# Two feed-forward down products: 16 of 22 k tiles by seven products in place of 8, with PSUM tiles of two banks

## The chip, the cores and the metric

The kernel runs on one core of one Trainium2 chip. The metric is the device time of one execution in microseconds, the median of three runs. A core has five engines with an instruction stream each: TensorE (PE, matmuls; PEld is its weight load), VectorE (DVE), ScalarE (ACT), GpSimd (POOL) and SyncE (SP). The last three also issue DMAs. Matmuls write to PSUM, eight banks of 512 fp32 numbers in each of 128 partitions; everything else lives in SBUF.

## The reference

One transformer block for 512 positions of width 1024, in fp32:

```
x = x + 0.5 * ffn(rmsnorm(x), up1, down1)        # FFN1
x = x + mixer(rmsnorm(x))                        # convolution and gated linear attention
x = x + 0.5 * ffn(rmsnorm(x), up2, down2)        # FFN2
return rmsnorm(x)

def ffn(y, up, down):                            # d_ff = 2816
    g, u = split(y @ up)                         # [512, 2816] each
    return (silu(g) * u) @ down                  # [512, 2816] @ [2816, 1024]
```

The change is about `@ down`, whose contraction has 2816/128 = 22 k tiles.

## The kernel before

**Precision.** A matmul of fp32 accuracy is made of three float32r products: every operand is split into a rounded part (`hi`) and the residue (`lo`), and hi·hi, hi·lo and lo·hi are added up in PSUM. Splitting a weight tile of 128 x 1024 takes a cast on ScalarE (`wh`, L358) and a subtraction on VectorE (`wl`, L359).

**Weights.** `Weights` streams all weights in the order of two lists, `PLAN` (tiles) and `STEPS` (uses). Each tile of 512 KB is fetched by SP's queue (L329) into the pool `f`; `take` returns the split tile of the next step and `issue` prepares two steps ahead. `wh` has three buffers, so the cast of a step waits until TensorE has done with a step three back.

**Seven products.** A 2 x 2 block product is computed by seven block products in place of eight (the Strassen–Winograd form), named m1, p2, q6, p5, q7, p3, p4. They need sums of weight blocks and of operand blocks. The weight sums are made by accumulating DMAs on POOL's queue (L333) and on VectorE (L343). The operand sums, in class `Operands`, are made on VectorE, and each operand is then split by L599 (ScalarE) and L600 (VectorE); `make` does that for one product. Class `Set` runs the seven products of one set on three banks: `a` takes p2, `b` takes m1, then q6, q7 and p4, which add onto what stands there, and `c` takes p5 and p3. Intermediate values that are used again (m1, q6, q7) are copied out of PSUM by ScalarE (L556) when their product ends. One product in a set is 24 matmuls of 256 columns (L551). `run_sets` takes the sets in a staggered order: the m1 of the next set comes between q7 and p4 of a set.

**Where it is used.** In the up products of both FFNs (9 sets each), in the mixer (12 sets and a tall one, L627), in 8 of the 22 k tiles of FFN1's down product (2 sets), and in 8 of the 22 of FFN2's. The rest goes by plain tiles: one k tile is 8 x 3 = 24 matmuls of 512 columns. FFN1's down product is 12 plain tiles (L386 to L388), two sets, and 2 plain tiles at the end (`TAIL1`). FFN2's is `last_down`, whose output has positions on the partitions: 10 plain tiles (L833 to L835), seven products of 24 matmuls of 512 columns (L884) in the order `CHUNK_ORDER`, and 4 plain tiles (`TAIL`). There each product uses two banks, and each result is added from PSUM into `X` by VectorE (`add`, L842). The evictions of the last tiles are L903.

**PSUM.** Pool `ps` has six tiles of one bank each, handed out by `MM()`; pool `pa` has two, handed out by `AUX()`. The order of the instructions on each engine comes from a scheduler that takes what is ready by the program's dependencies, tile by tile.

Of the kernel before, what the change touches and what calls it, by code (L numbers as in the profile page):

```python
# [42 lines left out]
TAIL1 = 2  # L43

# [70 lines left out]
def sets(mat, pairs):  # L115
    firsts = []
    for cols in pairs:
        firsts.append(len(PLAN))
        PLAN.extend((mat, 4 * j, 4, (c,), HW) for c in cols for j in range(2))
    STEPS.extend(order(firsts))  # L120
# [29 lines left out]
CHUNK_ORDER = ("m1", "p2", "q6", "p5", "q7", "p3", "p4")  # L150
CHUNK_STEP = {}


def last_plan(down):
    us = full(down, KF)
    units(us[CHUNK : KF - TAIL])
    firsts = []
    for s in range(2):
        firsts.append(len(PLAN))
        PLAN.extend((down, 4 * j + 2 * s, 2, (512 * i,), 512) for i in range(2) for j in range(2))  # L160
    CHUNK_STEP.update({(s, p): len(STEPS) + 2 * i + s for i, p in enumerate(CHUNK_ORDER)
                       for s in range(2)})
    STEPS.extend((n, p) for p in CHUNK_ORDER for n in firsts)
    units(us[KF - TAIL :])


def ffn_plan(up, down, plain, slow):

    units(group(up, KD, (0, DFF, P, DFF + P), slow))
    for f in range(2, plain):  # L170
        units(single(up, KD, f * P))
        units(single(up, KD, DFF + f * P))
    sets(up, [(s * HW, DFF + s * HW) for s in range(plain // 2, KF // 2)])
    if slow:
        us = full(down, KF)
        units(us[CHUNK : KF - TAIL1])
        sets(down, [(2 * s * HW, (2 * s + 1) * HW) for s in range(D // (2 * HW))])
        units(us[KF - TAIL1 :])
    else:
        last_plan(down)  # L180
    ENDS.append(len(STEPS))
# [34 lines left out]
def block_kernel(ctx: ExitStack, tc: tile.TileContext, xT, vecs, gf, gup, wgl, wts, out):  # L216
# [6 lines left out]
    ps = ctx.enter_context(tc.tile_pool(name="ps", bufs=6, space=bass.MemoryType.PSUM))  # L223
# [20 lines left out]

    def MM():
        cnt[0] += 1
        return ps.tile([P, S], F32, tag="mm", name=f"mm{cnt[0]}")
# [27 lines left out]
    class Weights:  # L275
# [14 lines left out]
        def phase(self, early, first=6):  # L290
# [4 lines left out]
            for i in range(lo, self.end):  # L295
                n, p = STEPS[i]
                if p == "m1" and i in CHUNK_STEP.values():
                    at = CHUNK_STEP[0, "m1"]
                    self.loads.setdefault(at - (4 if i == at else 2), []).append(n)
                    self.sums.setdefault(i, []).append(n)  # L300
# [9 lines left out]
            if self.end == len(STEPS):  # L310
                c = CHUNK_STEP
                for i, at in enumerate((c[1, "q6"], c[1, "p3"], c[1, "p3"], c[1, "p4"])):
                    self.pre.setdefault(at, []).append(STEPS[self.end - TAIL + i][0])
# [21 lines left out]
        def issue(self):  # L335
# [4 lines left out]
            for n in self.sums.get(at, ()):  # L340
                self.raw[n].append(tile_of("f", [P, 1024]))
                a11, a12, a21, a22, s3 = self.raw[n]
                nc.vector.tensor_tensor(out=s3, in0=a11, in1=a21, op=ALU.add)  # L343
                self.add(a21, a22)
# [6 lines left out]
            else:  # L351
                a11, a12, a21, a22, s3 = (self.raw[n] + [None])[:5]
# [174 lines left out]
    class Set:  # L527
# [9 lines left out]
        def run(self, p):  # L537
            b = {"m1": "b", "p2": "a", "q6": "b", "p5": "c", "q7": "b", "p4": "b", "p3": "c"}[p]
            fresh = b not in self.bank
# [19 lines left out]

    class Operands:  # L560
# [5 lines left out]
        def __init__(self, b):  # L566
            self.b = b
            self.parts = {}
            self.sums = set()
# [20 lines left out]
        def make(self, p):  # L590
# [5 lines left out]
            v = self.sum(p)  # L596
            h, l = (tile_of("op", [P, 1024], F32R) for _ in range(2))
# [5 lines left out]
        def get(self, p):  # L603
            return self.parts[p]

    class Tall:
# [7 lines left out]
        def run(self, p, s):  # L614
            b = {"p2": "a", "p5": "c", "p3": "c"}.get(p, "b")
            fresh = b not in self.bank
            if fresh:
                self.bank[b] = [MM(), MM()]
# [38 lines left out]
    def ffn(up, down, norm, nxt, plain, at):  # L657
# [28 lines left out]
        xo = Operands(normed)  # L686

        def plain_pair(f, g, u):
# [4 lines left out]
            mul(hid[:, f], s, t)  # L693
# [13 lines left out]

        def up_set(i):
            h = hid[:, plain + 2 * i : plain + 2 * i + 2]

            def done(s, p):
# [6 lines left out]
                if p == "q7":  # L718
                    u2 = T()
                    nc.vector.scalar_tensor_tensor(out=u2, in0=bank["c"], scalar=-1.0, in1=v["q7"],  # L720
                                                   op0=ALU.mult, op1=ALU.subtract)
                    s.u2 = u2
                if p == "p4":
                    nc.vector.scalar_tensor_tensor(
                        out=h[:, :, :HW], in0=pair(bank["b"]), scalar=-1.0, in1=pair(s.g1),
                        op0=ALU.mult, op1=ALU.mult)
                if p == "p3":
                    g2 = T()
                    nc.vector.tensor_tensor(out=g2, in0=bank["c"], in1=v["q6"], op=ALU.add)
# [24 lines left out]
        def banks():  # L754
            return [AUX(), AUX()] + [MM() for _ in range(KD - 2)]

        def mm(d, k, w, hl):
            c = slice(d * P, (d + 1) * P)
            mm3(o[d], w[0][:, c], w[1][:, c], hl[0][:, k % 2], hl[1][:, k % 2],
                k in (CHUNK, KF - TAIL1), k in (KF - TAIL1 - 1, KF - 1))  # L760
# [6 lines left out]
        ho = Operands(lambda j, l: hid[:, 4 * j : 4 * j + 4, l * HW : (l + 1) * HW])  # L767
        o = banks()
        hls = {k: split_hid(k) for k in (CHUNK, CHUNK + 2)}
        more = [4, 6, 8, 10, "m1", "p2", "p5", "q6", "q7", "p3"]  # L770
        for k in range(CHUNK, KF - TAIL1):
# [3 lines left out]
            if more:  # L775
                n = more.pop(0)
                if isinstance(n, int):
                    hls[CHUNK + n] = split_hid(CHUNK + n)
                else:
                    ho.make(n)  # L780
        for d in range(KD):
            add_half(d)
        ho.make("p4")
# [7 lines left out]
        def down_set(i):  # L791
            def done(s, p):
                for l, a, by in uses[p]:
                    xt = X[:, 4 * i + 2 * a : 4 * i + 2 * a + 2, l * HW : (l + 1) * HW]
# [4 lines left out]
            return Set(ho, done, keep=())  # L799

        run_sets(down_set)
# [18 lines left out]
    def last_down(us, hid, split_hid):  # L820
# [6 lines left out]

        o = [[MM(), MM()] for t in range(NTB - 1)] + [[AUX(), AUX()]]

        def mm(t, e, k, w, hl):  # L830
            wh, wl = (a[:, 512 * e : 512 * (e + 1)] for a in w)
            a, b = (v[:, k % 2, t * P : (t + 1) * P] for v in hl)
            nc.tensor.matmul(o[t][e], a, wh, start=k in (CHUNK, KF - TAIL), stop=False)  # L833
            nc.tensor.matmul(o[t][e], a, wl, start=False, stop=False)  # L834
            nc.tensor.matmul(o[t][e], b, wh, start=False, stop=k in (KF - TAIL - 1, KF - 1))  # L835
# [9 lines left out]
        ho = Operands(lambda j, l: hid[:, 4 * j : 4 * j + 4, l * HW : (l + 1) * HW])  # L845
        hls = {k: split_hid(k) for k in (CHUNK, CHUNK + 2)}
        more = [4, 6, 8, "m1", "p2", "p5", "q6", "q7", "p3"]
        for k in range(CHUNK, KF - TAIL):
            w = W.take(us[k])
            for t in range(NTB):  # L850
                for e in range(2):
                    mm(t, e, k, w, hls[k - k % 2])
            if more:
                n = more.pop(0)
                if isinstance(n, int):
                    hls[CHUNK + n] = split_hid(CHUNK + n)
                else:
                    ho.make(n)
# [3 lines left out]
        ho.make("p4")  # L862
# [6 lines left out]
        for p in CHUNK_ORDER:  # L869
            b = {"p2": "a", "p5": "c", "p3": "c"}.get(p, "b")  # L870
            fresh = b not in banks
            if fresh:
                banks[b] = [MM(), MM()]
            bh, bl = ho.get(p)
            for s in range(2):
                h, l = W.take()
                for i in range(2):
                    k = 2 * s + i
                    wh, wl = (a[:, 512 * i : 512 * (i + 1)] for a in (h, l))
                    for e in range(2):  # L880
                        c = slice(k * HW + e * P, k * HW + (e + 1) * P)
                        to = banks[b][e]
                        for n, (aa, ww) in enumerate(((bh, wh), (bh, wl), (bl, wh))):
                            nc.tensor.matmul(to, aa[:, c], ww,  # L884
                                             start=fresh and k == 0 and n == 0,
                                             stop=k == 3 and n == 2, skip_group_check=True)
# [618 lines left out]
```

## Time and profile before

| | us |
|---|---|
| median of three runs (1194.18 to 1195.4) | 1195.39 |
| the profiled execution | 1195.04 |
| its span, first to last instruction | 1193.3 |
| TensorE busy | 1183.7 |
| VectorE busy | 841.7 |
| ScalarE busy | 591.7 |
| GpSimd busy | 106.4 |

The span is what the trace covers; the profiled execution's own time holds 1.7 us more. Busy times of engines overlap. What sets the time is the chain of work that ended last, and an engine's idle time matters only where this chain runs through it. "Clock" is the TensorE clock that was granted, with 1 for full speed; it was 0.998 on average here.

### The profile page before, as it was taken

The numbers are of one execution on the slowest core, as the hardware profiler recorded it, in microseconds if no ns is written. First come the engines' busy times: TensorE is split into PE (matmuls) and PEld (weight loads), VectorE is DVE, ScalarE is ACT, GpSimd is POOL, SyncE is SP. The second block draws the span as 40 slices with busy tenths as digits, with TensorE's granted clock in tenths as the row PEclk, the third lists the DMA queues.
The fourth block names the chain that finished last, engine by engine and source line by source line (L and its number), as shares of the span: only waits on it lengthen the run. The fifth ranks groups of instructions, "written<-read, shape, count | busy, mean of one in ns | idle before, by whom it ended". The sixth has DMA issues, their size and how long they took to land.

```text
span 1193.3 us, 19134 instructions
## 1 busy us (share of the span) xinstructions
PE 1183.7 (99%) x7834; PEld 1091.4 (91%) x7834; DVE 841.7 (71%) x1010; ACT 591.7 (50%) x736; POOL 106.4 (9%) x143
## 2 busy tenths in 40 slices
PE   9999999999999999999999999999999999999997
PEld 8899999988988889999999998888889999998886
DVE  7976666854787976667787786555597656675675
ACT  6554454622452746464554574334355555562353
POOL 0011111000110110101111100100001111100100
PEclk9999999999999999999999999999999999999999
DMA  9477777633482767778666766602637777763431
GB/s 345 82 210 183 189 177 190 182 89 90 99 278 72 172 158 208 196 185 212 143 152 147 189 172 214 203 18 78 213 81 211 170 184 173 185 174 117 92 92 70
DMA packets 58471, 190.80 MB, mean 160 GB/s; under 512 B 6576, under 2 KB 10800, under 8 KB 58384
## 3 DMA queue, kind: packets, MB, share of 16 engines
q1 hardware_dynamic: 36912, 124.27, 30.5%
q0 software_dynamic: 16832, 60.83, 27.5%
q10 hardware_dynamic: 4640, 4.49, 1.2%
q8 instruction: 61, 1.00, 0.3%
q14 instruction: 26, 0.21, 0.1%
HBM read 124.55 MB, written 8.39 MB: 111 GB/s over the span
## 4 chain that ended last, share of the span: by engine, by line
PE 97%; DVE 2%; issue 1%; ACT 0%; POOL 0%; DVEq 0%; ACTq 0%; POOLq 0%
PE mm L551 52%; PE mm L410 7%; PE mm L388 6%; PE mm L386 6%; PE mm L387 6%; PE mm L627 3%; PE mm L884 3%; PE mm L834 2%; PE mm L835 2%; PE mm L833 2%; PE aux L1173 1%; DVE wl L359 1%; PE aux L386 1%; PE aux L835 1%; PE aux L388 1%; PE aux L834 1%
## 5 line engine op out<-in xcount | busy, mean ns | idle before, releaser
L551 PE MATMUL mm<-op,wh 128*128 128x256 f32 x3584 | 648.8, 284 | 0.0
L358 ACT CAST wh<-f 128x1024 fp32r<-128x1024 f32 (+1 forms) x325 | 339.4, 1046 | 459.0 <-PE mm L551 221.8
L551 PEld LDWEIGHTS mm<-op,wh 128*128 128x128 f32 x3584 | 559.0, 192 | 1.1
L359 DVE TENSOR_TENSOR wl<-f,wh 128x1024 fp32r<-128x1024 f32 (+1 forms) x325 | 394.8, 1219 | 210.9 <-ACT wh L358 205.9
L551 PE MATMUL mm<-op,wl 128*128 128x256 f32 x1792 | 507.5, 283 | 0.9 <-DVE wl L359 0.9
L551 PEld LDWEIGHTS mm<-op,wl 128*128 128x128 f32 x1792 | 343.3, 192 | 1.6 <-DVE wl L359 1.5
L333 POOL DMA_DIRECT2D f<-f x108 | 93.4, 867 | 932.1 <-DVE wl L359 483.1
L386 PE MATMUL mm<-op,wh 128*128 128x512 f32 x340 | 132.3, 389 | 0.0
L387 PE MATMUL mm<-op,wh 128*128 128x512 f32 x340 | 132.3, 389 | 0.0
L388 PE MATMUL mm<-op,wl 128*128 128x512 f32 x340 | 132.3, 389 | 0.0
L387 PEld LDWEIGHTS mm<-op,wh 128*128 128x128 f32 x340 | 63.8, 188 | 13.3
L388 PEld LDWEIGHTS mm<-op,wl 128*128 128x128 f32 x340 | 63.8, 188 | 13.2
L386 PEld LDWEIGHTS mm<-op,wh 128*128 128x128 f32 x340 | 63.8, 188 | 13.2
L410 PE MATMUL mm<-op,wh 128*128 128x512 f32 x256 | 64.5, 394 | 0.0
L410 PEld LDWEIGHTS mm<-op,wh 128*128 128x128 f32 x256 | 48.6, 190 | 10.4
L556 ACT COPY tp<-mm 128x512 f32<-128x512 f32 x90 | 52.2, 580 | 2.0 <-DVE tp L1323 2.0
L599 ACT CAST op<-hid 128x1024 fp32r<-128x1024 f32 x28 | 29.4, 1051 | 37.4 <-PE aux L834 20.7
L600 DVE TENSOR_TENSOR op<-hid,op 128x1024 fp32r<-128x1024 f32 x28 | 34.2, 1222 | 17.7 <-ACT op L599 17.6
L343 DVE TENSOR_TENSOR f<-f,f 128x1024 f32<-128x1024 f32 x36 | 44.0, 1223 | 0.8
L627 PE MATMUL mm<-wh,op 128*128 128x512 f32 x112 | 34.9, 389 | 0.0
L884 PE MATMUL mm<-wh,op 128*128 128x512 f32 x112 | 34.6, 389 | 0.0
L410 PE MATMUL mm<-op,wl 128*128 128x512 f32 x128 | 34.2, 389 | 0.0
(252 smaller groups left out, 1107.7 us busy)
## 6 DMA issues: line engine op xcount, KB each, us to landing
f<-wts SPq DMA_DIRECT2D x219, 512.0 KB, 4.4
f<-f POOLq DMA_DIRECT2D x108, 512.0 KB, 5.0
X<-xT SPq DMA_DIRECT2D x8, 256.0 KB, 5.3
xs<-X POOLq DMA_DIRECT2D x8, 256.0 KB, 5.5
ga<-tp ACTq DMA_DIRECT2D x8, 256.0 KB, 5.3
gb<-tp ACTq DMA_DIRECT2D x8, 256.0 KB, 5.3
tp<-ga SPq DMA_DIRECT2D x8, 256.0 KB, 5.9
tp<-gb SPq DMA_DIRECT2D x8, 256.0 KB, 3.0
```

Source lines behind the costliest of these rows:

```text
L333: nc.gpsimd.dma_start(out_, a, accum_op=ALU.add)
L343: nc.vector.tensor_tensor(out=s3, in0=a11, in1=a21, op=ALU.add)
L358: nc.scalar.copy(h[:, :w], raw[:, :w])
L359: nc.vector.tensor_tensor(out=l[:, :w], in0=raw[:, :w], in1=h[:, :w].bitcast(F32), op=ALU.subtract)
L386: nc.tensor.matmul(o, wh, ah, start=first, stop=False)
L387: nc.tensor.matmul(o, wh, al, start=False, stop=False)
L388: nc.tensor.matmul(o, wl, ah, start=False, stop=last)
L410: nc.tensor.matmul(o[c], w[:, s : s + P], a[k], start=k == 0 and j == 0, stop=k == kt - 1 and j == 2)
L551: nc.tensor.matmul(to, ww[:, s], aa[:, t], start=fresh and k == 0 and e == 0 and j == 0, stop=k == 3 and j == 2, skip_group_check=True)
L556: nc.scalar.copy(v, o)
L627: nc.tensor.matmul(self.bank[b][e], aa[:, c], ww, start=fresh and i == 0 and n == 0, stop=k == 3 and n == 2, skip_group_check=True)
L884: nc.tensor.matmul(to, aa[:, c], ww, start=fresh and k == 0 and n == 0, stop=k == 3 and n == 2, skip_group_check=True)
```

## The change

**FFN1's down product**: 4 plain tiles (`FILL1`), then two chunks of 8 k tiles by seven products (4 sets), then 2 plain ones. The operands of the second chunk, and the last three of the first, are made by hooks in the sets.

**The last down product**: 2 plain tiles (`FILL`), two chunks of 8 by seven products, 4 plain ones. The products come in a new order (`chunk_order`). Operand sums are accumulating DMAs on POOL's queue, from one part of `hid` to another (class `Signed`, L715); what must be subtracted is made with a negative sign, either in `hid` when it is written (`negative`) or when the operand is split. The evictions of p2, p3, q7 and p4 (all but the last p4) are done by `far`: ScalarE scales the bank into a tile (L1003), and an accumulating DMA on POOL's queue adds it to `X` (L1004, 256 KB). The others stay with VectorE (`add`, L997).

**PSUM**: pool `ps` has three tiles of two banks each, and `MM()` hands out their halves one after the other.

The rest of the diff is a mode `joint`, which is switched off in every place, and the forms that it needs.

```diff
+FILL1 = 4
-CHUNK_ORDER = ("m1", "p2", "q6", "p5", "q7", "p3", "p4")
+FILL = 2
+CHUNKS = 2
+def chunk_order():
+    seq = [(0, "m1"), (0, "p2")]
+    for c in range(CHUNKS):
+        seq += [(c, p) for p in ("p5", "p3", "q6", "q7")]
+        seq += [(c + 1, "m1"), (c, "p4"), (c + 1, "p2")] if c + 1 < CHUNKS else [(c, "p4")]
+    return seq
...
-    ps = ctx.enter_context(tc.tile_pool(name="ps", bufs=6, space=bass.MemoryType.PSUM))
+    ps = ctx.enter_context(tc.tile_pool(name="ps", bufs=3, space=bass.MemoryType.PSUM))
+    half_bank = []
+    def MM2():
+        cnt[0] += 1
+        half_bank.clear()
+        return ps.tile([P, 2, S], F32, tag="mm", name=f"mm{cnt[0]}")
     def MM():
-        cnt[0] += 1
-        return ps.tile([P, S], F32, tag="mm", name=f"mm{cnt[0]}")
+        if half_bank:
+            return half_bank.pop()
+        t = MM2()
+        half_bank.append(t[:, 1])
+        return t[:, 0]
...
-                self.raw[n].append(tile_of("f", [P, 1024]))
-                a11, a12, a21, a22, s3 = self.raw[n]
-                nc.vector.tensor_tensor(out=s3, in0=a11, in1=a21, op=ALU.add)
+                a11, a12, a21, a22 = self.raw[n]
+                if STEPS.index((n, "p2")) > STEPS.index((n, "q7")):
+                    self.raw[n].append(tile_of("f", [P, 1024]))
+                    nc.vector.tensor_tensor(out=self.raw[n][4], in0=a11, in1=a21, op=ALU.add)
                 self.add(a21, a22)
...
+                if p == "q7" and s3 is a11:
+                    nc.vector.tensor_tensor(out=a11, in0=a11, in1=a22, op=ALU.subtract)
...
+    class Signed(Operands):
+        ORDER = ("m1", "p2", "p5", "p3", "q6", "q7", "p4")
+        SUMS = {"m1": [((0, 0), (0, 1))], "p5": [((0, 0), (1, 1)), ((0, 1), (1, 1))],
+                "q6": [((1, 0), (0, 0))]}
+        def make(self, p):
...
+            if p in ("p2", "q6"):
+                nc.scalar.activation(hv, v, AF.Copy, scale=-1.0)
+                nc.vector.scalar_tensor_tensor(out=lv, in0=v, scalar=-1.0, in1=hv.bitcast(F32),
+                                               op0=ALU.mult, op1=ALU.subtract)
...
+            for to, a in self.SUMS.get(p, ()):
+                nc.gpsimd.dma_start(self.b(*to), self.b(*a), accum_op=ALU.add)
...
+            for l in range(2):
+                c = slice(l * HW, (l + 1) * HW)
+                nc.vector.scalar_tensor_tensor(out=hid[:, f, c], in0=s[:, c],
+                                               scalar=-1.0 if negative(f, l) else 1.0,
+                                               in1=t[:, c], op0=ALU.mult, op1=ALU.mult)
...
-        more = [4, 6, 8, 10, "m1", "p2", "p5", "q6", "q7", "p3"]
-        for k in range(CHUNK, KF - TAIL1):
+        more = ["m1", "p2", "p5", "q6"]
+        for k in range(FILL1):
...
+        makes = [(0, "q7"), (0, "p3"), (0, "p4")] + [(1, p) for p in Operands.ORDER]
+        run_sets(down_set, hooks={(i, p): [make] for i, ps in
+                                  ((0, ("m1", "q6", "q7")), (1, ("m1", "q6", "p5", "q7", "p4")),
+                                   (2, ("q6", "q7"))) for p in ps})
...
+        def far(t, e, bank, by):
+            xt = X[:, 4 * e : 4 * e + 4, t * P : (t + 1) * P]
+            v = T()
+            nc.scalar.activation(v, bank, AF.Copy, scale=by)
+            nc.gpsimd.dma_start(xt, blocks(v), accum_op=ALU.add)
...
             for l, e, by in uses[p]:
                 for t in range(2):
-                    add(2 * l + t, e, banks[b][t], by)
+                    (far if p in ('p2', 'p3', 'p4', 'q7') and (c, p) != seq[-1] else add)(2 * l + t, e, banks[b][t], by)
```

**How instructions move: TensorE in FFN1's up sets.** The place is the end of q7 of one set. In the rows, `mm` is a PSUM tile, `op` an operand (hi or lo), `wh` and `wl` the parts of a weight tile; the brackets hold the engines and DMA queues whose semaphores the instruction waits for. Before, `mm_718` is bank `b` of the set and `mm_946` that of the next set:

```order
484 L551 MATMUL mm_718<-op_605,wl_847 128x256
485 L551 MATMUL mm_946<-op_358,wh_877 128x256 [waits PE_49]
486 L551 MATMUL mm_946<-op_359,wh_877 128x256
487 L551 MATMUL mm_946<-op_358,wl_878 128x256 [waits DVE_49]
488 L551 MATMUL mm_946<-op_358,wh_877 128x256
489 L551 MATMUL mm_946<-op_359,wh_877 128x256
```

The m1 of the next set goes on for 24 matmuls, and p4 of the set (`mm_718` again, which waits for ScalarE) follows.

After, `mm_935` holds the banks `b` and `a` of the set, `mm_1091` its bank `c` and the next set's `b`, `mm_1221` the bank `a` of the next set's p2, and `wh_1161` that product's weights:

```order
615 L587 MATMUL mm_935<-op_596,wl_1062 128x256
616 L587 MATMUL mm_1221<-op_368,wh_1161 128x256 [waits Activation_49]
617 L587 MATMUL mm_1221<-op_369,wh_1161 128x256
618 L587 MATMUL mm_935<-op_666,wh_1129 128x256 [waits Activation_49]
619 L587 MATMUL mm_935<-op_667,wh_1129 128x256
620 L587 MATMUL mm_935<-op_666,wl_1130 128x256 [waits DVE_49]
```

Two matmuls of the next p2 stand between q7 and p4 now; the next m1 (into `mm_1091`) comes behind the first 12 matmuls of p4, when VectorE has read bank `c`. On ScalarE the cast of `wh_1161` is ahead of the copy of q7 for which p4 waits:

```order
76 L392 CAST wh_1129<-f_676 128x1024 [waits DMAHW5_49,PE_49,Activation_49]
77 L392 CAST wh_1161<-f_897 128x1024 [waits DMAHW7_49,DVE_49,PE_49]
78 L592 COPY tp_1157<-mm_935 128x512 [waits PE_49]
79 L392 CAST wh_1192<-f_672 128x1024 [waits DMASW1_49,DVE_49,PE_49]
80 L592 COPY tp_1190<-mm_1091 128x512 [waits DVE_49,PE_49]
```

Both the cast and the copy wait for TensorE, and the copy's turn comes after the cast.

**How instructions move: POOL in the last down product.** Before, POOL's queue ends with weight sums for the seven products (`f<-f`):

```order
134 L333 DMA f_11026<-f_11028 128x1024 [waits DMAHW2_49,DMAHW1_49,DMAHW7_49,DVE_49,Activation_49]
135 L333 DMA f_10949<-f_10953 128x1024 [waits DMASW6_49,DMAHW3_49,DMASW2_49,DVE_49]
136 L333 DMA f_11022<-f_11026 128x1024 [waits DMAHW7_49,DMASW7_49,DVE_49]
137 L333 DMA f_10951<-f_10949 128x1024 [waits DMAHW4_49,DMASW0_49,DVE_49]
138 L333 DMA f_11024<-f_11022 128x1024 [waits DMAHW0_49,DMASW1_49,DVE_49]
```

After, in the first chunk (`hid<-hid` are operand sums, `X<-tp` evictions: of p2 in rows 155 and 156, of p3 in rows 160 and 161):

```order
153 L715 DMA hid_8623<-hid_8623 128x4x256 [waits DMASW6_49,DVE_49]
154 L715 DMA hid_8623<-hid_8623 128x4x256 [waits DMASW6_49]
155 L1004 DMA X_7915<-tp_11089 128x4x128 [waits Activation_49]
156 L1004 DMA X_7915<-tp_11092 128x4x128 [waits DMASW1_49,PE_49,Activation_49]
157 L364 DMA f_11053<-f_11055 128x1024 [waits DMAHW6_49,DMAHW5_49,DVE_49]
158 L715 DMA hid_8623<-hid_8623 128x4x256 [waits DVE_49]
159 L715 DMA hid_8623<-hid_8623 128x4x256 [waits DMASW4_49,DMASW3_49]
160 L1004 DMA X_7915<-tp_11180 128x4x128 [waits DMASW5_49,Activation_49]
161 L1004 DMA X_7915<-tp_11183 128x4x128 [waits PE_49,Activation_49]
```

Operand sums, evictions and weight sums share one queue now, and a weight sum and two operand sums, each with waits of its own, stand ahead of p3's eviction.

More of the change, by code (lines that the diff above doesn't have):

```diff
@@ L175, in ffn_plan @@
         us = full(down, KF)
-        units(us[CHUNK : KF - TAIL1])
-        sets(down, [(2 * s * HW, (2 * s + 1) * HW) for s in range(D // (2 * HW))])
+        units(us[:FILL1])
+        sets(down, [(2 * s * HW, (2 * s + 1) * HW) for s in range(D // (2 * HW))],
+             range(FILL1, KF - TAIL1, CHUNK))
         units(us[KF - TAIL1 :])
@@ L617, in run @@
             if fresh:
+                half_bank.clear()
                 self.bank[b] = [MM(), MM()]
@@ L706, in ffn, with main, cross @@
             plain_pair(f, g, u)
+        def main(t):
+            return t[:, :, :HW] if xo.joint else pair(t)
+        def cross(t):
+            return t[:, :, HW:]
         def up_set(i):
-            h = hid[:, plain + 2 * i : plain + 2 * i + 2]
+            f = plain + 2 * i
+            h = hid[:, f : f + 2]
             def done(s, p):
```

214 lines of the change are left out of this document (154 added, 60 removed).

## The prediction

> **What bounds the kernel now.** I read the page's busy shares and clock first, then the waits of TensorE, then the chain that ended last.
>
> ```profile
> span 1193.3 us, 19134 instructions
> ...
> PE 1183.7 (99%) x7834; PEld 1091.4 (91%) x7834; DVE 841.7 (71%) x1010; ACT 591.7 (50%) x736; POOL 106.4 (9%) x143
> PEclk9999999999999999999999999999999999999999
> PE 97%; DVE 2%; issue 1%; ACT 0%; POOL 0%; DVEq 0%; ACTq 0%; POOLq 0%
> ```
>
> TensorE is busy for 99% of the span at a full clock, and 97% of the chain is its own work. The waits of TensorE, the whole answer:
>
> ```profile
> engine line waited for: us in total, times, longest us
> PE aux L260 <- POOL ones L257: 1.1, 1, 1.1
> PE mm L551 <- DVE wl L359: 0.9, 3, 0.6
> PE aux L1132 <- DVE qk L524: 0.5, 1, 0.5
> ```
>
> It waits 2.5 us in all. So each matmul removed is a gain at its full price, and each wait added is a loss at its full price, since no slack stands behind it. The prices of the matmuls are in the chain (start, us, work, count):
>
> ```profile
> 297.90 40.31 PE mm L551 x336
> ...
> 975.14 20.16 PE mm L551 x168
> ...
> 1126.34 38.08 PE mm L884 x168
> ...
> 1185.95 0.24 PE aux L835
> 1186.21 0.70 DVE X L903
> ```
>
> A matmul of 256 columns takes 40.31/336 = 0.1200 us; a whole set of seven products, 168 matmuls, takes 20.16. One of 512 columns takes 38.08/168 = 0.2267. TensorE ends at about 1186.2; the 7.1 us behind it are the same work before and after.
>
> **What is removed.** In FFN1's down product eight plain k tiles, 8 x 24 = 192 matmuls of 512 columns, become two sets more, 336 of 256: 192 x 0.2267 - 336 x 0.1200 = 43.5 - 40.3 = 3.2 us. In the last one eight plain tiles, 192 matmuls of 512, become seven products of 24 of 512: 24 x 0.2267 = 5.4. The gain is 8.6 us at most.
>
> **The PSUM tiles of two banks.** This edit is the smallest in the diff and reaches furthest. MM() now hands out halves of three two-bank tiles, and the order shows that a read of one half and a write of the other wait for each other. In each second set the next set's m1 now has the other half of the tile with the set's bank c, and waits until VectorE has read c, for which it needs the copy of q7. Before, after q7 come 24 matmuls of the next m1 (2.9 us), which cover the copy of q7 that p4 waits for. After, only 2 matmuls of the next p2 stand there, and the first of them waits for a weight cast that ScalarE does ahead of the copy. Rows of the timeline for these pieces (start, us, engine, operation):
>
> ```profile
> 206.59 1.05 ACT L358 CAST wh<-f 128x1024 fp32r<-128x1024 f32 x1 [1.79 <-PE mm L551]
> ...
> 207.54 0.58 ACT L556 COPY tp<-mm 128x512 f32<-128x512 f32 x1
> ...
> 208.81 0.68 DVE L720 SCALAR_TENSOR_TENSOR tp<-mm,tp 128x512 f32<-128x512 f32 x1
> ```
>
> The cast starts when TensorE frees its buffer (the releaser in the brackets is a matmul), so about at q7's end; the copy can start 207.54 - 206.59 = 0.95 later and takes 0.58. Against that stand 2 x 0.12 = 0.24 of matmuls: 0.95 + 0.58 - 0.24 = 1.29, and with 0.1 of handing over an estimated 1.4 us a place. Half of p4, 12 matmuls or 1.44 us, then covers the VectorE step of 0.68 for which the next m1 waits. The lower end is 0.34, where the cast has been done early (0.58 - 0.24); the upper 2.1, where the 0.68 is open too. I take 1.4, since the order on ScalarE is fixed: cast, then copy.
>
> The places, counted from the order: FFN1's up sets 6 x 1.4 = 8.4. FFN2's up sets 3 x 1.4 and 3 x 0.8, where transposes fill in: 6.6. The mixer's sets 7 x 1.4 = 9.8. ScalarE is busier there than in FFN1's up sets, as the windows show (from:to, us, then busy us of PE, PEld, DVE, ACT, POOL, then clock, DMA share, GB/s):
>
> ```profile
> 57.00:232.60 175.60, 175.57 (x1461) 175.51 (x1462) 122.13 (x123) 93.66 (x114) 19.83 (x23) 1.00 0.75 188
> 397.20:712.40 315.20, 314.00 (x2408) 301.93 (x2407) 242.37 (x299) 182.49 (x236) 34.04 (x43) 1.00 0.70 177
> ...
> 887.00:1071.90 184.90, 184.90 (x1546) 184.90 (x1545) 126.95 (x128) 101.87 (x127) 21.52 (x25) 1.00 0.74 182
> ```
>
> 182.5/315.2 is 58% against 53%, and VectorE 77% against 70%. I add two late casts there, 2.6 us, to 12.4. Single places in the convolution and the linear attention: 2. In all 8.4 + 6.6 + 12.4 + 2.0 = 29.4 us; by the bounds 7 to 46.
>
> **FFN1's down product.** The operands of the second chunk are made while the sets run, where before plain tiles hid them.
>
> ```profile
> 232.60:297.90 65.30, 65.30 (x290) 54.05 (x290) 34.18 (x33) 19.03 (x20) 3.45 (x4) 1.00 0.37 100
> 297.90:338.20 40.30, 40.30 (x337) 40.30 (x337) 29.08 (x32) 16.38 (x16) 3.44 (x5) 1.00 0.48 124
> ```
>
> The residue of an operand, from the groups by line (count, then busy us and mean ns):
>
> ```profile
> L600 DVE TENSOR_TENSOR op<-hid,op 128x1024 fp32r<-128x1024 f32 x28 | 34.2, 1222 | 17.7 <-ACT op L599 17.6
> ```
>
> The first row is the plain part: VectorE has 34.2 of 65.3 us to do, so half is free. The second is two sets: 29.1 of 40.3. Three sets need 29.08 x 1.5 = 43.6 us, and into three go ten makes and six operand sums, 16 x 1.222 = 19.5. That is 63.1 us of work beside 3 x 20.16 = 60.5 of matmuls: VectorE becomes the bound there. 2.6 us of surplus is the least if nothing is ready ahead; work ahead can take it to 1, and makes put in front of a residue that TensorE waits for can bring 8. I take 5, between, as each make of 1.2 us comes as one lump ahead of weight residues. With one two-bank place of 1.4: -3.2 + 5 + 1.4 = +3.2 us.
>
> **The last down product.** In the order of before no two products on one bank followed each other; now p5 and p3 do, q6 and q7, and at the end q7 and p4. A product on a bank just used waits for its evictions. An eviction pair in the timeline:
>
> ```profile
> 1136.76 1.28 DVE L842 SCALAR_TENSOR_TENSOR X<-mm,X 128x512 f32<-128x512 f32 x2
> ```
>
> The issue of a DMA on POOL, from the groups by line, and the DMAs' landing (operation, count, KB, median us from issue):
>
> ```profile
> L333 POOL DMA_DIRECT2D f<-f x108 | 93.4, 867 | 932.1 <-DVE wl L359 483.1 <-DVE f L343 315.7 <-DVE st_q L518 25.2
> ```
>
> ```profile
> f<-f POOLq DMA_DIRECT2D x108, 512.0 KB, 5.0
> ...
> xs<-X POOLq DMA_DIRECT2D x8, 256.0 KB, 5.5
> ```
>
> p5 to p3, twice: two evictions 1.28, and 0.26 from the last matmul's start to an eviction's (1185.95 to 1186.21 above): 1.5 each, 3.0.
>
> q6 to q7: q6's eviction on VectorE adds into the block of X into which p3 went, and p3 now goes there by a scale on ScalarE and an accumulating DMA. That DMA's two halves are free at 0.58 and 1.16 after p3, take 0.87 to issue and, by the nearest row (256 KB on the same queue), 5.5 to land: 7.5 us. With the second eviction of 0.64 it is 8.2, against q6's own 24 x 0.2267 = 5.44: 2.7, with a hop 2.9. So in the last chunk. In the first, two DMAs of operand sums stand ahead on POOL: 2 x 0.87 more gives 4.7, and these wait for VectorE and for earlier ones first: I take 5.5, of 1.5 to 8. On VectorE the residues of the next weights and operands are queued behind that eviction, so the wait isn't made good elsewhere. [...]
>
> q7 to p4 at the end: two scales on ScalarE, 1.16 less 0.24 of cover: 0.9. The start: m1 and p2 come after only 2 plain tiles, and the evictions of those stand behind an operand residue (1.22) that waits for an operand sum by DMA: 1.6, of 0 to 5.5. The tail: half 1 of three two-bank tiles waits for the eviction of half 0, three times 0.7 and a hop: 2.8. Sum 3.0 + 5.5 + 2.9 + 0.9 + 1.6 + 2.8 = 16.7; less 5.4 it is +11.3.
>
> The rest I cost at nothing. `Signed` turns VectorE's operand sums into eight DMAs on POOL's queue; VectorE has room for the signs that it gets instead: the two halves of `hid` as two multiplies in FFN2's up sets, where it is busy for 127.0 of 184.9 us, and the in-place weight difference of q7, one of 1.22, where before stood a sum of the same size. If that room is gone, they come to some 1.2 us a set. POOL issues for only 106 us of the span, so what its queue costs is the order of its waits, which is in the 5.5 above.
>
> **The sum.** 29.4 + 3.2 + 11.3 = 43.9 us. The profiled execution took 1195.04 us, 0.35 below the median of 1195.39: 1195.0 + 43.9 = 1238.9, and 1239.3 against the median.
>
> **The rivals.** *A: faster.* TensorE's order stays, and ScalarE, busy for 50%, has the casts and copies done before TensorE is there; the accumulating DMAs land within their product. Then the gain of 8.6 stays: 1195.4 - 8.6 = 1186.8. It decides where the waits come to less than 8.6 us over some 35 places, under 0.25 each. For it: idle time of ScalarE, and not one wait of TensorE for it before. Against: a copy of q7 can't start ahead of q7's end, and 0.58 us is more than two matmuls. 5%.
>
> *B: the sets keep their cover.* The waits on half tiles are covered by work that runs meanwhile, and only FFN1's VectorE load and the last product's waits count: 1239.3 - 29.4 - 1.4 = 1208.5. For it: in FFN2's sets transposes fill in, and the list of instructions gives TensorE 12 to 24 other matmuls near each place. [...] Against: the order shows the semaphore, whatever the memory could do. 15%.
>
> *C: stops feed on each other.* The three cast buffers are filled when TensorE frees them; when it stops, the next cast starts late as well, and each place costs 2.8 instead of 1.4 over 21 places: 29 us more, 1268. The same time comes if VectorE, at 77% in the mixer, falls behind. [...] 12%.
>
> *The forecast*, with the places and prices as summed: 68%. Its own bounds, 0.9 to 2.0 a place and 1 to 8 for the two large waits, reach from 1222 to 1260.
>
> **How the numbers follow.** Predicted 1239.3. The range takes in B and the forecast, 83%: from 1205 to 1262. A measurement of this kernel can tell about 0.2%, 2.4 us, from no change. Faster by more: A, 5%. Within it, between A and B: 1%. Slower: the rest, 94%.
>
> **What would show it.** In the waits of TensorE: matmuls of the sets behind ScalarE's copy or cast, 15 to 25 times at 1.2 to 1.6 us; matmuls of the last chunks behind VectorE's or ScalarE's evictions, two of them over 2.5 us; busy VectorE over 95% in FFN1's first three down sets. The accumulating DMAs of X should land after 4 us or more. Wrong would be: no row of ScalarE among TensorE's waits (B or A), waits of the sets over 2 us (C), or the time of TensorE's matmuls itself changed by anything but 8.6 us.

## The result: 11.7% slower

The changed kernel takes 1334.64 us (1329.86 to 1338.3, 4 runs) against 1194.95, a ratio of 1.117 with a 95% interval of 1.113 to 1.121. The forecast was slower, 1239.3, in a range up to 1262: the direction held, the size did not; 140 us were added where 44 were worked out. The page of the profiled execution after:

```profile
span 1334.9 us, 19566 instructions
...
PE 1224.5 (92%) x7954; PEld 1117.4 (84%) x7954; DVE 872.3 (65%) x1048; ACT 617.4 (46%) x768; POOL 144.6 (11%) x177
...
PEclk9989999999999999898999999999989998988799
```

Two things are new. TensorE stands still for 1334.9 - 1224.5 = 110 us where it was 10. And it is busy for 1224.5 us with work that would take 1183.7 - 8.6 = 1175 at the old rates, 49 us less. 101 + 49 - 8.6 is the difference of the spans. Part of the 49 is a slower clock: in the stretches where the granted clock is 0.50, ahead of the tail, TensorE is busy for 62.6 us, and by estimate half of that, 31 us, is lost (in 86:90 below, 16 matmuls of 256 columns take 3.73 us, 0.23 each, where 0.12 was the price before). This does not account for the other 18, and they were not followed. What TensorE waits for, the longest rows of the answer (in total, times, longest):

```profile
PE mm L587 <- DVE tp L847: 27.0, 8, 4.5
PE mm L1053 <- DVE X L997: 24.2, 4, 19.5
PE mm L587 <- ACT wh L392: 14.1, 14, 1.8
PE mm L587 <- DVE tp L1496: 7.3, 5, 2.9
PE mm L988 <- DVE tp L872: 6.2, 1, 6.2
...
PE mm L988 <- DVE X L1073: 2.6, 3, 1.1
```

The third row (1.0 us each) and the last (the tail, 2.6 where 2.8 was worked out) are the waits on two-bank tiles that were forecast. The first, for the addition that starts g1 (L847) in the up sets, was not forecast; the second was, at 5.5. By stages (busy us of PE, PEld, DVE, ACT, POOL, then clock, DMA share, GB/s), the first row from the kernel before, the others after:

```profile
50.40:232.40 182.00, 181.82 (x1513) 181.52 (x1513) 128.16 (x129) 98.21 (x118) 21.55 (x25) 1.00 0.74 184
...
50.40:265.50 215.10, 193.39 (x1521) 189.22 (x1520) 129.89 (x132) 97.57 (x117) 21.57 (x25) 0.97 0.62 152
265.50:379.10 113.60, 110.62 (x799) 104.18 (x797) 92.71 (x102) 49.70 (x52) 11.94 (x17) 1.00 0.56 143
...
432.60:777.50 344.90, 323.70 (x2401) 307.77 (x2400) 241.46 (x301) 181.25 (x234) 33.15 (x42) 0.98 0.63 157
...
958.50:1177.40 218.90, 200.18 (x1555) 195.54 (x1554) 128.25 (x131) 101.40 (x125) 26.30 (x29) 0.95 0.65 156
1177.40:1334.90 157.50, 116.52 (x474) 92.02 (x472) 88.36 (x116) 63.20 (x86) 33.44 (x29) 0.89 0.68 130
```

| stage | before, us | after, us | change | forecast |
|---|---|---|---|---|
| FFN1 up | 182.0 | 215.1 | +33.1 | +8.4 |
| FFN1 down | 116.5 | 113.6 | -2.9 | +3.2 |
| mixer | 315.2 | 344.9 | +29.7 | +12.4 |
| FFN2 up | 184.9 | 218.9 | +34.0 | +6.6 |
| last down and end | 121.6 | 157.5 | +35.9 | +11.3 |

The stretches between them added 11.8. The up products, whose arithmetic the change does not touch, lost 67 us, about as much as both down products and the mixer together, and VectorE has hardly more to do there than before (129.9 us against 128.2 in FFN1's). So it is VectorE's queue that stands still. Its waits say for what; in the kernel before, none of VectorE's waits is for a DMA:

```profile
DVE f L386 <- DMA f<-f: 45.9, 13, 6.0
DVE X L997 <- DMA X<-tp: 20.4, 4, 17.2
```

L386 is the in-place weight difference of q7, `a11 - a22`. One of the places in time (start, us, instruction, in brackets the idle time before it and what ended it):

```profile
78.22 1.23 DVE L393 TENSOR_TENSOR wl<-f,wh 128x1024 fp32r<-128x1024 f32 x1 [0.32 <-ACT wh L392]
83.99 1.23 DVE L386 TENSOR_TENSOR f<-f,f 128x1024 f32<-128x1024 f32 x1 [4.55 <-DMA f<-f]
85.14 0.68 DVE L847 TENSOR_TENSOR tp<-mm,tp 128x512 f32<-128x512 f32 x1
```

```profile
77.55 0.86 POOL L364 DMA_DIRECT2D f<-f  x1 [8.49 <-DVE wl L393]
```

```profile
85.97 0.77 PE L587 MATMUL mm<-op,wh 128*128 128x256 f32 x2 [3.94 <-DVE tp L847]
```

The accumulating DMA that adds a11 onto a12 (p2's weights, which so become p3's) is issued at 77.55. The difference overwrites a11, which this DMA reads, so it waits for its landing; behind it in VectorE's queue stands the addition of L847, which has long had its data, and TensorE waits for that one. The two matmuls then take 0.77 us, where two in one row took 0.40 ahead of the stop (76.83 to 81.51): the clock in 86:90 is 0.50 (clock is the third number from the end):

```profile
82.00:86.00 4.00, 0.06 (x2) 0.06 (x1) 2.01 (x3) 0.14 (x1) 0.00 (x0) 0.83 0.18 34
86.00:90.00 4.00, 3.73 (x16) 3.43 (x17) 3.29 (x4) 2.05 (x3) 0.00 (x0) 0.50 0.46 134
90.00:94.00 4.00, 4.00 (x30) 4.00 (x30) 0.16 (x1) 1.24 (x2) 0.13 (x1) 0.82 0.36 132
...
1225.00:1244.00 19.00, 0.00 (x0) 0.00 (x0) 1.40 (x3) 1.99 (x2) 4.81 (x4) 0.58 0.92 158
1244.00:1247.00 3.00, 2.88 (x7) 2.33 (x8) 2.25 (x2) 0.00 (x0) 0.46 (x1) 0.50 0.31 59
```

The lower two rows are the stop of 19.5 us before q7 in the last down product. There POOL's queue is what stands:

```profile
1216.13 3.32 POOL L715 DMA_DIRECT2D hid<-hid  x1
1233.49 1.28 POOL L715 DMA_DIRECT2D hid<-hid  x1 [14.04 <-DMA hid<-hid]
1234.29 3.09 POOL L1004 DMA_DIRECT2D X<-tp  x2
```

The second operand sum waits 14 us for the first to land, and p3's two evictions (L1004) stand behind it; q6's eviction waits for those.

### The profile page after: what moved, and what is told of

It is laid out like the page before. It is cut to its first block, busy times and chain, and to the rows that moved or that the text cites. A ratio compares the mean times of both kernels' runs of the same rounds, so it can differ in the third digit from the quotient of the medians.

```text
span 1334.9 us, 19566 instructions
## 1 busy us (share of the span) xinstructions
PE 1224.5 (92%) x7954; PEld 1117.4 (84%) x7954; DVE 872.3 (65%) x1048; ACT 617.4 (46%) x768; POOL 144.6 (11%) x177
## 5 line engine op out<-in xcount | busy, mean ns | idle before, releaser
L587 PE MATMUL mm<-op,wh 128*128 128x256 f32 x3808 | 714.5, 290 | 58.2 <-DVE tp L847 27.0
L587 PEld LDWEIGHTS mm<-op,wh 128*128 128x128 f32 x3808 | 609.0, 196 | 70.6 <-issue 40.6
L393 DVE TENSOR_TENSOR wl<-f,wh 128x1024 fp32r<-128x1024 f32 (+1 forms) x337 | 409.1, 1218 | 252.5 <-ACT wh L392 247.5
L587 PE MATMUL mm<-op,wl 128*128 128x256 f32 x1904 | 543.7, 288 | 3.3 <-DVE wl L393 3.2
L587 PEld LDWEIGHTS mm<-op,wl 128*128 128x128 f32 x1904 | 371.2, 196 | 5.7 <-DVE wl L393 5.4
L420 PE MATMUL mm<-op,wh 128*128 128x512 f32 x292 | 114.5, 395 | 2.1 <-DVE y L558 2.1
L422 PE MATMUL mm<-op,wl 128*128 128x512 f32 x292 | 114.2, 392 | 0.7 <-DVE wl L393 0.7
L421 PE MATMUL mm<-op,wh 128*128 128x512 f32 x292 | 114.4, 392 | 0.0
L1053 PE MATMUL mm<-wh,op 128*128 128x512 f32 x224 | 73.2, 405 | 24.4 <-DVE X L997 24.2
L386 DVE TENSOR_TENSOR f<-f,f 128x1024 f32<-128x1024 f32 x36 | 44.0, 1223 | 50.9 <-DMA f<-f 45.9
L1053 PEld LDWEIGHTS mm<-wh,op 128*128 128x128 f32 x224 | 43.7, 195 | 35.8 <-issue 21.7
L420 PEld LDWEIGHTS mm<-op,wh 128*128 128x128 f32 x292 | 55.3, 189 | 16.3 <-DVE y L558 3.4
L422 PEld LDWEIGHTS mm<-op,wl 128*128 128x128 f32 x292 | 55.1, 189 | 12.8 <-DVE wl L393 1.1
L444 PE MATMUL mm<-op,wh 128*128 128x512 f32 x256 | 64.4, 391 | 0.9 <-DVE X L911 0.8
L421 PEld LDWEIGHTS mm<-op,wh 128*128 128x128 f32 x292 | 55.2, 189 | 11.3
L444 PEld LDWEIGHTS mm<-op,wh 128*128 128x128 f32 x256 | 47.9, 189 | 11.9 <-issue 1.5
L1053 PE MATMUL mm<-wl,op 128*128 128x512 f32 x112 | 44.9, 401 | 0.0
L739 PE MATMUL mm<-wh,op 128*128 128x512 f32 x112 | 34.9, 389 | 0.0
```

Source lines behind the costliest of these rows:

```text
L386: nc.vector.tensor_tensor(out=a11, in0=a11, in1=a22, op=ALU.subtract)
L393: nc.vector.tensor_tensor(out=l[:, :w], in0=raw[:, :w], in1=h[:, :w].bitcast(F32), op=ALU.subtract)
L420: nc.tensor.matmul(o, wh, ah, start=first, stop=False)
L421: nc.tensor.matmul(o, wh, al, start=False, stop=False)
L422: nc.tensor.matmul(o, wl, ah, start=False, stop=last)
L444: nc.tensor.matmul(o[c], w[:, s : s + P], a[k], start=k == 0 and j == 0, stop=k == kt - 1 and j == 2)
```

## The experiments

Theory P: the two-bank tiles cost nearly all that lies outside the last down product. Theory S, formed after the first four runs: the in-place difference does. In the last product, Q: the stop is p3's DMA in POOL's queue; H: the operand sums by DMA are late themselves. Ratios are to the kernel before, with 95% intervals.

**Two-bank tiles alone**, on the kernel before:

```diff
-    ps = ctx.enter_context(tc.tile_pool(name="ps", bufs=6, space=bass.MemoryType.PSUM))
+    ps = ctx.enter_context(tc.tile_pool(name="ps", bufs=3, space=bass.MemoryType.PSUM))
```

`MM()` hands out halves and calls `half_bank.clear()` as in the change.

> The kernel before with one edit: the PSUM pool of three two-bank tiles and MM() that hands out halves, as in the changed kernel. Theory P (the two-bank tiles cost nearly all that was added outside the last down product, some 105 of 140 us: half-tile waits, and a halved clock after the long ones): 1290 to 1305 us, TensorE waiting behind VectorE and ScalarE in the up sets of both FFNs and in the mixer, granted clock about 0.975. Rival W (weight sums, operand sums and DMAs of the new products delay the sets): within 5 us of 1195, no such waits.

1232.09 us, 1.031 (1.029 to 1.033): +37.5, a third of what P asked for. The waits are the ones forecast, most of them of 1.0 us, none longer than 1.8:

```profile
PE mm L561 <- ACT wh L368: 11.3, 11, 1.6
PE mm L561 <- ACT tp L566: 4.0, 3, 1.8
PE mm L846 <- DVE X L918: 2.4, 3, 0.8
```

**Single banks**, on the changed kernel: `bufs=6`, and `MM()` returns one bank.

> The changed kernel with one edit taken back: six PSUM tiles of one bank each, all else as it is. Theory P: 1225 to 1235 us, what is left over 1195 lies in the last down product alone. Rival W: over 1310, the waits in the up sets stay.

1253.72 us, 1.049 (1.047 to 1.051). Between the two theories: 81 us less, but the up sets still stop, behind VectorE's residues now (12.9 us, 10 times), with VectorE waiting for DMAs ahead of the in-place difference (65.4 us, 19 times). P falls; something else sits in the sets.

**FFN1's down product alone**, on the kernel before (the diff's hunks for `FILL1`, `sets`, `operands(f)`, the hooks):

> The kernel before with FFN1's part of the change alone (two chunks by seven products, operands made in the sets; single banks, old last down product). The prediction's term (VectorE short by 2.6 us or more in the first three sets): 1197 to 1200. Rival (VectorE and ScalarE keep up, as the changed kernel's FFN1 down stage suggests, which went from 116.5 to 113.5 us between the starts of its neighbours): 1191.5 to 1192.5, 3.2 us less.

1191.63 us, 0.9973 (0.9962 to 0.9983): 3.0 us less, the arithmetic's full gain. In the three sets VectorE is busy for 54.8 of 60.4 us:

```profile
253.60:314.00 60.40, 60.40 (x505) 60.40 (x504) 54.83 (x59) 30.46 (x30) 6.03 (x7) 1.00 0.62 155
```

**Single banks, all evictions by VectorE** in the last down product:

```diff
-                    (far if p in ('p2', 'p3', 'p4', 'q7') and (c, p) != seq[-1] else add)(...)
+                    add(2 * l + t, e, banks[b][t], by)
```

> As the one with single banks, and in the last down product every eviction is VectorE's add onto X, none by ScalarE and an accumulating DMA. Theory Q (the 19.5 us stop before q7 is q6's eviction waiting for p3's accumulating DMA, which stands in POOL's queue behind operand sums that wait): at least 20 us less than the one with single banks. Rival H (the operand sums by DMA are late themselves, and the products would stop for their operands in any case): less than 8 us less, and the stop shows up behind an operand's residue.

1246.03 us, 1.043 (1.041 to 1.045): 7.7 less than single banks. The stop before q7 shrinks from 14.9 to 3.3. In the profiled executions the last product, from its first plain tile on, is 10.7 us shorter (148.4 to 137.7), while the stages before it, which the edit does not touch, are 4.4 longer. So 7.7 is in H's range, but the stage itself lies between H (under 8) and Q (20 or more), and this run does not decide.

**The in-place difference alone**, on the kernel before:

```diff
-                self.raw[n].append(tile_of("f", [P, 1024]))
-                nc.vector.tensor_tensor(out=s3, in0=a11, in1=a21, op=ALU.add)
...
+                if p == "q7" and s3 is a11:
+                    nc.vector.tensor_tensor(out=a11, in0=a11, in1=a22, op=ALU.subtract)
```

> The kernel before with one edit: in the sets (not in the last down product) the weights of q7 are no longer a sum made ahead into a tile of their own, but are made in place (a11 minus a22) at q7's turn, as in the changed kernel. Theory S (this subtraction waits for the accumulating DMAs that read and write a11, and VectorE's queue stands behind it): the kernel with single banks lost some 34 us in the stages of the sets, so about 1225 to 1232 us here, with TensorE waiting behind VectorE's residues. The prediction's value (one subtraction where one sum stood, hidden): 1195.

1240.62 us, 1.038 (1.036 to 1.040), with 34 differences. They include the last set of each of the four series of sets (both FFNs' up products, FFN1's down product, the mixer), whose p2 comes after q7, so that p3 gets other weights than the reference's. Without these four, 30 differences as in the change:

> The kernel before with one edit: q7's weights made in place at q7's turn, in those sets where the changed kernel does it (not in the mixer's tall one, which keeps its sum made ahead, and not in the last down product). Theory S: the difference that single banks showed (1253.7 against 1221.2 with sums ahead), 32 us: 1224 to 1230 us, TensorE waiting 12 to 15 us behind VectorE's residues and the clock below 0.99. The prediction's value: 1195.

The sets left out are these four, not the tall one, whose p2 comes before q7. 1233.42 us, 1.032 (1.030 to 1.034): +38.8, a little above the range. S holds, and the prediction's zero is refuted. A late difference into a tile of its own was not run; what points to the write in place is that a DMA's landing ends the wait of 19 of the 30. TensorE's main wait, and VectorE's:

```profile
PE mm L555 <- DVE wl L363: 20.0, 15, 2.4
```

```profile
DVE f L356 <- DMA f<-f: 67.7, 19, 5.3
```

**Two-bank tiles, sums ahead**, on the changed kernel: the sum a11 + a21 is made ahead into its own tile in all sets again (the last down product keeps its differences in place).

> The changed kernel with q7's weight sum made ahead into its own tile again in all sets, two-bank tiles kept. Theory S with P (the two edits make each other worse, and the waits over 3 us that halve the clock come from both together): the sets then cost only the 37 us of two-bank tiles alone, and the last down product its 28 to 36: 1255 to 1268 us, and no wait over 2.5 us in the up sets. If the long waits are from the two-bank tiles: over 1300.

1263.57 us, 1.057 (1.055 to 1.059): 71 us less by this one line, as S said. The longest wait left in the sets is 1.6 us. **Both put right:** single banks, sums ahead.

> The changed kernel with six single banks and q7's weight sum made ahead in all sets: what is left of the change is FFN1's down product and the last down product. Theory S with P: 1195 - 3 + 27 = 1219 us, from 1215 to 1224; all that is left over the kernel before lies in the last down product. If a part is still missing: over 1230.

1221.22 us, 1.022 (1.020 to 1.023). The sets are as before; all that is left is in the last down product.

**p3's eviction by VectorE**, otherwise the same: `'p3'` left out of the list for `far`.

> As the one with single banks and sums ahead, but p3's eviction in the last down product is VectorE's add, so that q6's eviction, into the same block of X, need not wait for a DMA that stands behind operand sums in POOL's queue. Theory Q: the stop of 15 us before q7 goes, 10 to 14 us less than with it: 1205 to 1210. Rival H (the operands themselves are late by their sums' DMAs): 0 to 6 us less, the stop moves to an operand's residue.

1215.66 us, 1.017 (1.015 to 1.019): 5.6 less, so H, not Q in full. The stop before q7 shrank to 2.9, but others are left:

```profile
PE mm L1051 <- ACT wh L390: 6.7, 1, 6.7
PE mm L986 <- DVE tp L870: 6.4, 1, 6.4
PE mm L1051 <- DVE X L995: 3.2, 2, 2.9
```

The second row is an operand that waits for its sum: VectorE's queue stood behind a residue whose cast (L705) waited 7.9 us for a DMA `hid<-hid`. The first is a weight cast that waited for weight sums by DMA.

**Operand sums by VectorE** in place of DMAs, then also all evictions by VectorE, then p3's by DMA again:

```diff
-                nc.gpsimd.dma_start(self.b(*to), self.b(*a), accum_op=ALU.add)
+                nc.vector.tensor_tensor(out=self.b(*to), in0=self.b(*to), in1=self.b(*a), op=ALU.add)
```

> As the one with single banks, sums ahead and p3 by VectorE, and the operand sums of the last down product are VectorE's adds in place instead of accumulating DMAs on POOL's queue. Theory H (what is left, stops of 6 to 7 us at the first plain tile and in the second chunk with the halved clock behind them, is operands waiting for their sums' DMAs, one after the other): 1191 to 1197 us, no wait of TensorE over 3 us. Rival V (VectorE is then the bound, with eight sums of 1.22 more): 1203 to 1210, many waits of 1 to 2 us behind VectorE's residues.

> As the last, and no eviction goes by ScalarE and DMA: all are VectorE's adds. If VectorE has room (H): within 3 us of the last. If VectorE is the bound (V): p2's, q7's and p4's eight or more adds of 0.64 each cost 4 to 9 us.

> As the one with VectorE's operand sums, but p3's eviction is by ScalarE and DMA again, as in the changed kernel. POOL's queue now holds no operand sums. Theory Q in its full form (the 15 us stop was POOL's queue standing still behind an operand sum that waited for another's landing): the stop shrinks to the DMA's own time, about 3 us in each chunk, so 4 to 8 us above the one without it. If the DMA itself is what costs: 12 us or more above it.

1197.32 us, 1.0024 (1.0015 to 1.0034); 1196.83, 1.0017 (1.0008 to 1.0027); 1198.33, 1.0031 (1.0021 to 1.0041). The operand sums by DMA cost 18 us with p3 by VectorE (1215.66 to 1197.32) and 23 with p3 by DMA (1221.22 to 1198.33). The stop at the first plain tile is gone; that behind a weight cast stays (4.9 in the first of the three). With the sums gone, evictions by DMA cost or bring about 1 us; that p3's would still cost 4 was wrong.

**What is left in the last product.** On the version with everything by VectorE (1196.83): weight sums ahead in its chunks too, and then the old order of products with the old operands as well:

```diff
-        seq += [(c, p) for p in ("p5", "p3", "q6", "q7")]
+        seq += [(c, p) for p in ("q6", "p5", "q7", "p3")]
-        return Signed(lambda j, l: ...)
+        return Operands(lambda j, l: ...)
```

> As the one with all evictions and operand sums by VectorE, single banks, and q7's weights made ahead in the last down product's chunks too: nothing is made in place any more. If what is left there (TensorE behind ScalarE's weight casts, 5 us) is the in-place difference waiting for DMAs: 1190 to 1193. If it is the new order: no change, 1195 to 1198.

> As the last, with the products of each chunk in the order of before (q6, p5, q7, p3: no two on one bank in a row) and the operands made as in the kernel before. If the order is what costs: 1187 to 1190 us, the full 8.6 saved or nearly. If VectorE is the bound with sums and evictions of two chunks: 1192 or more, waits behind VectorE's residues.

1202.43 us, 1.0065 (1.005 to 1.008): worse by 5.6 (against 1196.83), where one expectation had 4 or more of gain and the other no change. There is one stop of 10.0 us behind a weight cast, which itself waited 10.7 us for an accumulating DMA of weights (`f<-f`); why that DMA comes so late stays open. And 1191.08, 0.9969 (0.9956 to 0.9981): order and operands together bring 11. This version is 16 of 22 k tiles by seven products in both down products, and it beats the kernel before; but the last down product gives hardly any of its 5.4 us, as FFN1's alone stands at 1191.63. In its two chunks VectorE is busy for 74.4 of 80.3 us, and their 336 matmuls, 76.2 us at 0.2267 each, take 4.1 longer:

```profile
1079.70:1160.00 80.30, 77.86 (x337) 62.64 (x338) 74.36 (x81) 41.63 (x41) 6.89 (x8) 1.00 0.55 137
```

**Two-bank tiles and the in-place difference together**, on the kernel before:

> The kernel before with just two edits: two-bank tiles, and q7's weights made in place in the sets. If the excess comes from these two together: 1300 to 1320 us, waits over 3 us behind VectorE's additions in the up sets, with the clock at half behind them. If it needs the other parts: 1271, the sum of 37.5 and 39.

1295.10 us, 1.084 (1.082 to 1.086): +100, between the two expectations. Alone they cost 37.5 + 38.8 = 76.3; 24 us come from their meeting. In the profiled executions some 15 of these are idle time of TensorE and some 9 busy time. The waits are the changed kernel's; the addition L730 here is L847 there:

```profile
PE mm L565 <- DVE tp L730: 24.7, 8, 4.1
PE mm L565 <- ACT wh L372: 13.7, 14, 1.6
```

## Why the prediction was wrong

The ladder: 1194.95 + 100 (both edits of the sets) - 3.0 (FFN1's down) + 34.5 (the last product on two banks: 1263.57 - 1232.09 with the 3.0 added back) = 1326.6, of 1334.64. Some 8 us stay without a run of their own; the four runs spread over 8.4.

**The two-bank tiles: right in kind.** Worked out 29.4 in the sets, 1.4 in FFN1's down product and 2.8 in the tail, 33.6; alone they cost 37.5. Of 14 waits behind ScalarE 11 end with the cast, which stands ahead of the copy; no run changed that order. That the sum came so close is in part luck: these waits are fewer and shorter (15.3 us in all, about 1.1 each, where I had 1.4), and TensorE's busy time grew by 14.5 us (1183.7 to 1198.2), of which I had nothing. Rival B, that the waits on half tiles would be covered, is refuted by the same run.

**The step that failed: "the in-place weight difference of q7, one of 1.22, where before stood a sum of the same size", costed at nothing.** It measured 38.8 us alone and about 63 beside the two-bank tiles (1295.10 - 1232.09). I compared its duration and VectorE's free time; both were right and neither mattered. The old sum read tiles that had been loaded and wrote a fresh one. The new one overwrites a tile that an accumulating DMA still reads, so it gets that DMA's landing as a wait, 3.6 us on average (67.7 us in 19 waits), and everything queued behind it on VectorE gets it too. I also placed it in the last down product; the condition in the diff makes it apply to every set whose p2 comes before q7, that is, to all but the last of each of the four series: 32 of the 36 differences lie outside the last down product.

**FFN1's down product: wrong sign.** I forecast +3.2 and saw a gain of 3.0. VectorE's 63.1 us in three sets were mis-sized: 54.8 were measured. I had 16 pieces of 1.22 in the three sets, and the timeline has 12, eight operand residues and four operand sums; the others came earlier. The two old sets from which I scaled also held a residue for the plain tiles behind them.

**The last down product: right places, sizes off.** Forecast +11.3; +34.5 on two banks, 29.6 on single ones (1221.22 - 1191.63). p5 to p3 (1.5 each) and the tail (2.6 for 2.8) came as worked out; q6 to q7 in the last chunk was 1.7 for 2.9, q7 to p4 0.2 for 0.9. The stop before q7 was 19.5 for 5.5: I counted two issues of 0.87 ahead of p3's eviction, while one of them waited 14 us for the landing of the sum before it. But that stop was not alone: with p3 by VectorE only 5.6 us were won, and the term that I lacked is that operand sums by DMA, each waiting for the one before, cost 18 to 23 us together. The start was 6.2 for 1.6 for the same reason: the cast ahead of it waited 8.2 us for an operand sum.

**Rival C and the clock.** C's sign, waits of the sets over 2 us, is there, but not by C's causes, casts that start late or a VectorE with too much to do: the waits for casts are 1.0 us on average, and VectorE stood still behind a DMA. The half clock cost some 31 us by the estimate above, which no sum had: the clock was 0.50 in 86:90, right behind a stop of 3.94 us, and 0.50 as well behind a stop of 1.78 us, as told below.

**The landing of the DMAs.** X's evictions landed in 7.9 us and the operand sums of 512 KB in 6.9 (medians of the changed kernel), so even the nearest row of before, 5.5, was too short.

## What to carry to other kernels

When an edit lets an instruction write in place, its price is not its duration (1.23 us here) but the transfers that still read or write the tile (3.6 us on average in 19 waits), and then what stands behind it in its engine's queue (3.94 us of TensorE at the place above): look up who touches the tile, and what stands behind the instruction. A chain of DMAs that each wait for the last one's landing held back the transfers behind it on the shared queue: p3's evictions stood behind a wait of 14.04 us. The same sums on VectorE, at 1.2 us each, were cheaper here by 18 to 23 us. And waits can cost more together than apart: here 24 us more, some 15 of it idle time of TensorE and some 9 busy time, at a granted clock of 0.983 where the two edits alone had 0.995 and 0.993.

## What the runs showed of the hardware

- The granted clock was 0.50 behind stops of TensorE, long ones and a short one. In the changed kernel 14 stretches at 0.50 lie ahead of the tail, the shortest of 3.41 us, the longest of 20.48; the first three start at 84.60, 111.91 and 159.70. In the kernel with two-bank tiles alone, TensorE stands still for 1.78 of the 3.40 us of the first row below, the clock is 0.50 in the second row and 1.00 in the third. With the in-place difference alone, it stands still for 1.07 us in one row and 1.15 in the next, and the clock is 1.00 in both and in the row behind them (busy us of PE first; clock third from the end):

```profile
52.10:55.50 3.40, 1.62 (x14) 1.42 (x13) 2.70 (x5) 3.40 (x5) 1.74 (x2) 1.00 0.64 120
55.52:58.90 3.38, 3.38 (x18) 3.38 (x17) 2.27 (x3) 0.10 (x1) 0.00 (x0) 0.50 1.07 189
58.94:62.30 3.36, 3.36 (x30) 3.32 (x29) 2.91 (x4) 2.64 (x3) 0.00 (x0) 1.00 0.81 311
```

```profile
983.02:986.42 3.40, 2.33 (x20) 2.13 (x18) 1.84 (x3) 0.00 (x0) 0.00 (x0) 1.00 0.02 4
986.44:989.80 3.36, 2.21 (x18) 2.21 (x19) 3.36 (x4) 3.19 (x5) 0.00 (x0) 1.00 0.32 111
989.84:993.20 3.36, 3.09 (x26) 2.88 (x25) 2.49 (x3) 1.82 (x3) 0.00 (x0) 1.00 0.61 199
```

  So at these two places the time that TensorE stood still does not tell whether the clock drops; what decides it was not shown.
- The accumulating DMAs of `hid` (rows of 1 KB) and of `X` (rows of 512 bytes) landed later, in 6.9 and 7.9 us, than those of whole weight rows, in 5.5. The landing times in the changed kernel (operation, count, KB, median us):

```profile
f<-f POOLq DMA_DIRECT2D x120, 512.0 KB, 5.5
hid<-hid POOLq DMA_DIRECT2D x8, 512.0 KB, 6.9
X<-tp POOLq DMA_DIRECT2D x14, 256.0 KB, 7.9
```

  Whether the short rows are the reason is not shown. Once the operand sums were VectorE's, the same evictions of X (all 14, p3's among them) landed in 5.9, and the weight sums of that whole run in 4.9; with p3 by VectorE as well, the other 10 evictions landed in 8.6. So the median of such a DMA varied by half, 5.9 to 8.6, between kernels with the same rows.
